# A hybrid decoder step on one core: fillers in every pause of TensorE's start, and two loads on another queue

## The chip, the cores and the metric

The kernel runs on one core of one Trainium2 chip. The metric is the time of one execution on the device, in microseconds (us), as the median of several runs. TensorE (PE) multiplies matrices, VectorE (DVE) and ScalarE (ACT) work elementwise, GpSimd (POOL) does the small rest, and the queues of SyncE (SP) and of ScalarE can issue transfers (DMA).

## The reference

One inference step of a decoder layer for a prompt of 512 rows and 32 sampled rows (8 sequences of 4), each row 1024 wide, in float32. What matters here is the front of the layer and the size of what follows:

```python
shift, scale, gate = jnp.split(jax.nn.silu(c) @ w_cond + b_cond, 3, axis=-1)
h = x * (1 + scale[:, None]) + shift[:, None]
return gate, split_columns(h @ w_in)          # w_in: 1024 x 11280
...
yA = dilated_attention(...)                   # 3 groups of 8 heads, then combined by their softmax sums
yB = gated_delta(short_conv(qkv_b), ...)      # 8 heads of 128
merged = sigmoid(g_a) * (yA @ w_branch_a) + sigmoid(g_b) * (yB @ w_branch_b)
y = LayerNorm(ALPHA * x + gate * (merged @ w_out))
```

It also returns the new key and value caches, the convolution rows and the delta states.

## The kernel before

**Products in three parts.** A float32 product of `h` with a weight tile is made of three rounded ones: each operand is split into a high part (ScalarE's copy to float32r) and a low part (VectorE's subtraction). `hhi`, `hlo` are those of `h`; `whi`, `wlo` or `hi`, `lo` those of a weight tile `wt`. One tile of `h @ w_in` is 8 blocks of 128 rows (`k`) x 3 products x 2 halves of 272 columns, into banks of PSUM called `pp` (two), or `pg` (three), `pb` (one), `pd` (two).

**The front.** `h` depends on `c`. `cT` (the transposed conditioning vectors) is loaded, ScalarE's `th` (tanh) and two instructions of VectorE make `cs` from it, which is silu(c). Then for each of the 8 blocks `k`: a group of 8 matmuls `pd<-wm,cs` with the block `wm[k]` of `w_cond`; ScalarE's copy `Y`; two small matmuls `pd<-cst,Y`, which transpose it; VectorE's `mod` adds the bias `mb` (from `bT`) and scales `xT[k]`; ScalarE's `hhi` and VectorE's `hlo` split it. As soon as a block of `h` is there, the matmuls of the first three weight tiles (`ahead`) use it, six a tile.

The loads of the front all stand in SP's queue, in this order, with their size in KB: `cT` 128, `bT` 12, `wm0` 1024, `cst` 165, `xT` 544, `wm1` 1024, `wt` 512, `wm2` 1024, `xT` 544, `wt` 512, `wm3` 1024, `wt` 512, `wm4` 1024, `xT` 544, `wm5` 1024, `wm6` 1024, `xT` 544, `wm7` 1024: 12,209 KB (12.5 MB) in all. `wm2` ends 4,433 KB (4.5 MB) into it.

**The order.** The kernel is recorded first: every operation goes into a list with its reads and writes (`Recorder.add`; all instructions therefore have one line, L707, in the profile). `Recorder.schedule` then plays the list through with costs in microseconds and, at each planned moment, gives each engine the ready operation of the best rank. What it writes down is the order of the instructions on each engine; the chip keeps to that order, and waits on semaphores for real.

**Fillers.** `Recorder.warm` puts a matmul of ones (`warm<-ones`, 128x128, float32, into a spare bank) into TensorE's order where the planner sees a pause of at least `GAP` = 0.25 us. It refuses where the planned busy time of the last 3.413 us (`heat`) is over `HEAT` = 3.0 us:

```python
heat = sum(b - max(a, at - 3.413) for a, b in busy[-400:] if b > at - 3.413)
if heat > self.HEAT:
    return None
```

**Further on.** Two things that the prediction speaks of: a `za` job (one weight tile, evacuated in two halves by ScalarE's `spare<-pp` or `zt<-pp` and VectorE's `spare<-spare,pp` or `zt<-zt,pp`, which frees the bank), and the combination of the three attention groups: weights `R` are made on VectorE and ScalarE, stored to a DRAM tile `dw`, loaded again, spread over partitions, as `wv`, and multiplied on VectorE into `ya` and `NB`. While that goes on the large caches are copied from DRAM to DRAM by the same queue (`out_kv_s<-in_cache`).

Of the kernel before, what the change touches and what calls it, by code (L numbers as in the profile page):

```python
# [245 lines left out]
class Recorder:  # L246
# [4 lines left out]
    OVER = {"ve": 0.08, "se": 0.10, "ge": 0.05}  # L251
    AGAIN = {"pe": 0.0, "ve": 0.11, "se": 0.14, "ge": 0.11, "sp": 0.0}
    HOLD = 1.0
    GAP, HEAT = 0.25, 3.0
    ENTER = {(128, 128): 0.197, (64, 128): 0.197, (64, 64): 0.142, (32, 32): 0.073, (128, 64): 0.1, (128, 32): 0.0,
             (64, 32): 0.1, (32, 128): 0.2, (32, 64): 0.1}
    ENGINES = ("pe", "ve", "se", "ge", "sp")
# [397 lines left out]
    def warm(self, wait, avail, at, best, busy, state):  # L655

        if avail or best is None or best[0] < at or best[1] == "pe" and best[0] <= at:
            return None
        if wait and wait[0][0] < at + self.GAP:
            return None  # L660
        heat = sum(b - max(a, at - 3.413) for a, b in busy[-400:] if b > at - 3.413)
        if heat > self.HEAT:
            return None
        for pool, tag in self.spare:
            key = (id(pool), tag)
            s = state.get(key)
            if not pool.open or s is None or not s["slots"] or s["wait"] or min(s["slots"]) + self.WAKE["pe"] > at:
                continue
            v = pool.tile([128, 512], F32, name="warm", tag=tag)
            v.base.bufs = pool.bufs  # L670
            self.rank, self.group = 40, None
            op = self.add("pe", "matmul", (v[:, 0:128], self.ones, self.ones), dict(start=True, stop=True))
            self.rank = 0
            t = v.base
            t.turn, t.left, t.line, t.given = {}, 1, None, True
            t.free = max(s["slots"].pop(s["slots"].index(min(s["slots"]))), pool.since)
            for x in (t, self.ones.base):
                x.pool.left += 1
            self.ones.base.left += 1
            op.left, op.banks, op.ready, op.group = 0, [t], at, None  # L680
            self.warmed = getattr(self, "warmed", 0) + 1
            return op
        return None
# [76 lines left out]
def body(ctx, tc, io):  # L760
    rec = Recorder()
    pe, ve, se, ge, sp = rec.engines()
# [94 lines left out]
    with ExitStack() as fctx:  # L857
        fr = pool(fctx, "front", 1)
        cT = fr.tile([128, KT, 32], F32, name="cT")
        sp.dma_start(cT, io["cT"])  # L860
        bT = fr.tile([128, 24], F32, name="bT")
        sp.dma_start(bT, io["bT"])
        th = fr.tile([128, KT, 32], F32, name="th")
        se.activation(th, cT, AF.Tanh, scale=0.5)
        ve.tensor_scalar(th, th, 0.5, 0.5, op0=OP.mult, op1=OP.add)
# [1164 lines left out]
    at = [0, 0, 9, 9, 18, 18, 27, 27]  # L2030
# [311 lines left out]
```

## Time and profile before

| | |
|---|---|
| median of 3 runs | 927.26 us (926.62 to 927.31) |
| the profiled execution | 929.9 us, of which the span of instructions is 928.1 us |
| TensorE busy | 907.1 us, 98% of the span |
| VectorE, ScalarE busy | 737.6 us (79%), 435.2 us (47%) |
| fillers | 17 instructions, the last before 21.5 us |
| mean granted clock of TensorE | 0.993 |

The profile is of one execution. A row of a timeline has the start and the duration in us, the engine, the line, the operation with its output and inputs, how many instructions are merged in the row, and in brackets the idle time before it with what ended it. A row of windows has, after the stretch and its length, the busy time of PE, PEld (weight loads), DVE, ACT and POOL with the number of instructions, the granted clock, the share of the DMA engines and GB/s. A float32 matmul shows as two rows.

### The profile page before, as it was taken

Reading aid. Unit: us, or ns where it says so; the run is one execution under the profiler, and the core shown is the slowest. Engines: PE = TensorE matmul, PEld = TensorE weight load, DVE = VectorE, ACT = ScalarE, POOL = GpSimd, SP = SyncE. Lnnn points to the kernel's source line nnn. Section 1 sums busy time; section 2 is a strip of 40 time slices with the busy share of each in tenths; the row PEclk is TensorE's granted clock in tenths of the full one; section 3 lists DMA queues with packets and bytes.
Section 4 is the critical chain, followed back from the end, with each engine's and each line's share of the span. In section 5 each row is a group of like instructions: output and inputs, shape, how many; then the busy total and the mean of one; then the engine's idle time right before and its main releaser. Section 6 shows DMA issues by size and latency. Waiting matters only on the chain.

```text
span 928.1 us, 20971 instructions
## 1 busy us (share of the span) xinstructions
PE 907.1 (98%) x8168; PEld 847.6 (91%) x8168; DVE 737.6 (79%) x1635; ACT 435.2 (47%) x1007; POOL 78.7 (8%) x187
## 2 busy tenths in 40 slices
PE   8999999999999999999999999999999999999895
PEld 6899999999998999998999998988999999997684
DVE  3486668587679999999999977466899989857658
ACT  3374636656355756446766445422532222245311
POOL 0131011120000130001120000020010000000000
PEclk9999999999999999999999999999999999999998
DMA  9776677477787779898779685479699999989613
GB/s 359 290 206 220 190 233 234 148 222 230 204 262 231 268 234 299 269 319 267 262 256 292 189 278 209 122 243 378 209 312 364 329 406 387 345 286 316 227 41 116
DMA packets 104569, 237.89 MB, mean 256 GB/s; under 512 B 29891, under 2 KB 61261, under 8 KB 100757
## 3 DMA queue, kind: packets, MB, share of 16 engines
q1 hardware_dynamic: 104468, 236.55, 76.2%
q8 instruction: 64, 1.05, 0.5%
q14 instruction: 37, 0.30, 0.1%
HBM read 220.49 MB, written 103.70 MB: 349 GB/s over the span
## 4 chain that ended last, share of the span: by engine, by line
PE 79%; DVE 11%; DMA 5%; ACT 2%; issue 2%; SPq 0%; DVEq 0%; ACTq 0%
PE pp L707 55%; PE pg L707 11%; PE pd L707 8%; PE pb L707 3%; DVE r L707 2%; DVE lo L707 2%; DVE slab L707 1%; DMA wt<-in_w_in 1%; DMA wm<-in_w_mod 1%; DVE tmp L707 1%; DVE Tb L707 1%; DMA wv<-dw 1%; DMA rb<-dr 1%; ACT L707 1%; DMA dO<-vr 1%
## 5 line engine op out<-in xcount | busy, mean ns | idle before, releaser
L707 PE MATMUL pp<-hhi,hi 128*128 128x272 f32 x1360 | 399.9, 294 | 2.0 <-DVE spare L707 2.0
L707 PE MATMUL pp<-hhi,lo 128*128 128x272 f32 x1360 | 401.7, 295 | 0.0
L707 PE MATMUL pp<-hlo,hi 128*128 128x272 f32 x1360 | 400.3, 294 | 0.0
L707 PEld LDWEIGHTS pp<-hhi,hi 128*128 128x128 f32 x1360 | 257.1, 189 | 4.6 <-DVE spare L707 2.3
L707 PEld LDWEIGHTS pp<-hlo,hi 128*128 128x128 f32 x1360 | 257.3, 189 | 2.2 <-issue 1.3
L707 PEld LDWEIGHTS pp<-hhi,lo 128*128 128x128 f32 x1360 | 257.0, 189 | 2.1 <-issue 1.0
L707 ACT ACTIVATE hi<-wt 128x1024 fp32r<-128x1024 f32 (+1 forms) x102 | 104.6, 1026 | 183.8 <-PE pp L707 150.9
L707 DVE TENSOR_TENSOR lo<-wt,hi 128x1024 fp32r<-128x1024 f32 (+1 forms) x102 | 119.9, 1176 | 34.9 <-ACT hi L707 34.2
L707 DVE SCALAR_TENSOR_TENSOR acc<-ext,cw,acc 128x568 f32<-128x568 f32 x72 | 57.3, 799 | 5.2 <-ACT acc L707 4.9
L707 ACT ACT_TABLE_LOAD x38 | 48.8, 1283 | 4.1 <-DVE acc L707 2.7
L707 DVE TENSOR_REDUCE slab<-slab 128x8 f32<-128x512 f32 (+2 forms) x66 | 42.7, 654 | 0.2
L707 DVE TENSOR_TENSOR slab<-slab 128x512 f32<-128x512 f32 (+1 forms) x66 | 42.8, 665 | 0.1
L707 ACT ACTIVATE P<-P,st 128x256 f32<-128x256 f32 (+1 forms) x64 | 31.2, 489 | 20.8 <-DVE st L707 20.6
L707 POOL COPY cx<-ext 128x3 f32<-128x3 f32 (+1 forms) x48 | 32.3, 703 | 70.8 <-ACT ext L707 70.7
L707 ACT ACTIVATE zt<-pp 128x272 f32<-128x272 f32 x48 | 18.7, 389 | 41.0 <-PE pp L707 32.1
L707 PE MATMUL pp<-ybl,hi 128*128 128x272 f32 x128 | 37.1, 290 | 0.0
L707 PE MATMUL pp<-ybh,lo 128*128 128x272 f32 x128 | 37.0, 289 | 0.0
L707 PE MATMUL pp<-ybh,hi 128*128 128x272 f32 x128 | 36.9, 288 | 0.0
L707 PE MATMUL pg<-k,q 128*128 128x128 f32 (+1 forms) x192 | 35.7, 309 | 0.0
L707 PEld LDWEIGHTS pg<-k,q 128*128 128x128 f32 x192 | 27.8, 191 | 3.0 <-issue 1.4
L707 ACT ACTIVATE q<-pp 64x272 f32<-64x272 f32 (+1 forms) x48 | 26.3, 549 | 8.5 <-PE pp L707 8.0
L707 DVE CUSTOM_DVE_ANT_0 P<-pg,bias 128x256 f32<-128x256 f32 (+1 forms) x64 | 24.0, 401 | 3.7 <-PE pg L707 3.3
(408 smaller groups left out, 1673.4 us busy)
## 6 DMA issues: line engine op xcount, KB each, us to landing
out_kv_s<-in_cache SPq DMA_DIRECT2D x144, 512.0 KB
wt<-in_w_in SPq DMA_DIRECT2D x88, 512.0 KB
out_kv_s<-in_cache SPq DMA_DIRECT2D x24, 496.0 KB
wm<-in_w_mod SPq DMA_DIRECT2D x8, 1024.0 KB
slab<-in_ks SPq DMA_DIRECT2D x32, 256.0 KB
slab<-in_vs SPq DMA_DIRECT2D x32, 256.0 KB
kv<-in_ks SPq DMA_DIRECT2D x16, 512.0 KB
kv<-in_vs SPq DMA_DIRECT2D x16, 512.0 KB
```

The costliest lines, as they stand in the source:

```text
L707: getattr(real[x.engine], x.name)(*map(arg, x.args), **{k: arg(v) for k, v in x.kw.items()})
```

## The change

A constant `FULL` = 17.0 is added: before 17 us of planned time, the limit on `heat` no longer holds, so that every pause of at least 0.25 us gets a filler. And the two loads of `cT` and `bT` are issued by ScalarE instead of SP.

```diff
-    GAP, HEAT = 0.25, 3.0
+    GAP, HEAT, FULL = 0.25, 3.0, 17.0
...
         heat = sum(b - max(a, at - 3.413) for a, b in busy[-400:] if b > at - 3.413)
-        if heat > self.HEAT:
+        if heat > self.HEAT and at > self.FULL:
             return None
...
         cT = fr.tile([128, KT, 32], F32, name="cT")
-        sp.dma_start(cT, io["cT"])
+        se.dma_start(cT, io["cT"])
         bT = fr.tile([128, 24], F32, name="bT")
-        sp.dma_start(bT, io["bT"])
+        se.dma_start(bT, io["bT"])
```

The planner's times move with it, and so the order of the instructions on every engine, to the end of the program. Of TensorE's matmuls only the fillers change in number: 29 instead of 17.

TensorE at the start of the program, before:

```order
L707 MATMUL warm<-ones 128x128 x8
L707 MATMUL pd<-wm,cs 32x256 x8
L707 MATMUL warm<-ones 128x128
L707 MATMUL pd<-cst,Y 128x9 x2
L707 MATMUL pd<-wm,cs 32x256 x8
L707 MATMUL warm<-ones 128x128 x4
L707 MATMUL pp<-hhi,whi 128x272 x2
L707 MATMUL warm<-ones 128x128 x2
L707 MATMUL pd<-cst,Y 128x9 x2
```

TensorE at the same place, now:

```order
L707 MATMUL warm<-ones 128x128 x12
L707 MATMUL pd<-wm,cs 32x256 x8
L707 MATMUL warm<-ones 128x128 x2
L707 MATMUL pd<-cst,Y 128x9 x2
L707 MATMUL warm<-ones 128x128 x7
L707 MATMUL pd<-wm,cs 32x256 x8
L707 MATMUL warm<-ones 128x128 x3
L707 MATMUL pp<-hhi,whi 128x272 x2
L707 MATMUL warm<-ones 128x128 x2
L707 MATMUL pd<-cst,Y 128x9 x2
```

Four more fillers stand ahead of the first group, one more behind it, seven new ones ahead of the second group, and one fewer behind that.

VectorE where the weights `R` of the attention groups are finished, before (this is near 590 us in the profile):

```order
L707 RECIPROCAL Z<-Z 128x128
L707 TENSOR_TENSOR R<-R,Z 128x256
L707 SCALAR_TENSOR_TENSOR spare<-spare,pp 128x272
L707 TENSOR_TENSOR lo<-wt,hi 128x1024
L707 SCALAR_TENSOR_TENSOR ya<-ya,spare 128x512
L707 SCALAR_TENSOR_TENSOR S<-S,etot,pd 128x128
L707 RECIPROCAL rn<-rn 128x4
L707 TENSOR_TENSOR vr<-pd,rn 128x512
L707 SCALAR_TENSOR_TENSOR zt<-zt,pp 128x272
```

VectorE at the same place, now:

```order
L707 TENSOR_TENSOR lo<-wt,hi 128x1024
L707 SCALAR_TENSOR_TENSOR spare<-spare,pp 128x272
L707 SCALAR_TENSOR_TENSOR ya<-ya,spare 128x512
L707 RECIPROCAL rn<-rn 128x4
L707 TENSOR_TENSOR vr<-pd,rn 128x512
L707 TENSOR_TENSOR R<-R 128x256
L707 SCALAR_TENSOR_TENSOR zt<-zt,pp 128x272
L707 TENSOR_TENSOR Z<-R 128x128
L707 RECIPROCAL Z<-Z 128x128
L707 TENSOR_TENSOR R<-R,Z 128x256
```

The last step of `R` stood ahead of `lo`, `ya` and `vr`; now it stands behind them and behind one `zt`.

VectorE a little later, where the products with `wv` meet the evacuation of the `za` jobs, before (near 610 us):

```order
L707 TENSOR_TENSOR ya<-ya,wv 128x4x4x32
L707 SCALAR_TENSOR_TENSOR spare<-spare,pp 128x272
L707 TENSOR_TENSOR NB<-NB,wv 128x4x4x32
L707 TENSOR_TENSOR ya<-ya,NB 128x512
L707 TENSOR_TENSOR ya<-ya,wv 128x4x4x32
L707 TENSOR_TENSOR nd<-nd,cum 128x256
L707 TENSOR_TENSOR NB<-NB,wv 128x4x4x32
L707 TENSOR_TENSOR nd<-nd,cd 128x256
L707 TENSOR_TENSOR lo<-wt,hi 128x1024
L707 SCALAR_TENSOR_TENSOR spare<-spare,pp 128x272
```

VectorE at the same place, now:

```order
L707 SCALAR_TENSOR_TENSOR spare<-spare,pp 128x272
L707 TENSOR_TENSOR nd<-nd,cum 128x256
L707 TENSOR_TENSOR nd<-nd,cd 128x256
L707 TENSOR_TENSOR ya<-ya,wv 128x4x4x32
L707 TENSOR_TENSOR lo<-wt,hi 128x1024
L707 SCALAR_TENSOR_TENSOR spare<-spare,pp 128x272
L707 TENSOR_TENSOR NB<-NB,wv 128x4x4x32
L707 SCALAR_TENSOR_TENSOR spare<-spare,pp 128x272
L707 TENSOR_TENSOR ya<-ya,NB 128x512
```

Between the first job's two evacuations (`spare<-spare,pp`) there stood three products with `wv`, a sum, two `nd` and a `lo`; now there stand two `nd`, one product with `wv` and the `lo`.

## The prediction

> **What bounds the kernel now.** I read the page's head first, then the chain of waits, then the first 20 us of TensorE in order of time, and last the two places where TensorE stops later on.
>
> From the page:
>
> ```profile
> span 928.1 us, 20971 instructions
> PE 907.1 (98%) x8168; PEld 847.6 (91%) x8168; DVE 737.6 (79%) x1635; ACT 435.2 (47%) x1007; POOL 78.7 (8%) x187
> PE 79%; DVE 11%; DMA 5%; ACT 2%; issue 2%; SPq 0%; DVEq 0%; ACTq 0%
> ```
>
> TensorE is busy for 98% of the span and holds 79% of the chain that ended last. Time is won by giving it real work earlier, or by letting it run at full speed for longer. A busy share does not say which: a filler counts as busy, and so does a matmul at half speed. So I read the start, TensorE alone in order of time (start, duration, what, count):
>
> ```profile
> 1.05 3.78 PE L707 MATMUL warm<-ones 128*128 128x128 f32 x16 [1.05 <-DVE ones L707]
> 6.94 1.94 PE L707 MATMUL pd<-wm,cs 128*32 128x256 f32 x16 [2.11 <-DMA wm<-in_w_mod]
> 9.40 0.99 PE L707 MATMUL pd<-cst,Y 128*128 128x9 f32 x4
> 11.18 1.94 PE L707 MATMUL pd<-wm,cs 128*32 128x256 f32 x16 [0.79 <-DMA wm<-in_w_mod]
> 13.05 2.08 PE L707 MATMUL warm<-ones 128*128 128x128 f32 x8
> 15.38 1.05 PE L707 MATMUL warm<-ones 128*128 128x128 f32 x4
> 16.22 0.86 PE L707 MATMUL pd<-cst,Y 128*128 128x9 f32 x4
> 16.94 0.63 PE L707 MATMUL pp<-hhi,wlo 128*128 128x272 f32 x2
> 17.75 1.07 PE L707 MATMUL pd<-wm,cs 128*32 128x256 f32 x16
> 19.38 0.61 PE L707 MATMUL pd<-cst,Y 128*128 128x9 f32 x4
> 20.81 0.61 PE L707 MATMUL warm<-ones 128*128 128x128 f32 x4
> ```
>
> Each float32 matmul leaves two rows, so x16 is eight instructions. The same group `pd<-wm,cs` takes 1.94 us at 6.94 and at 11.18 and 1.07 us at 17.75; a filler takes 0.47 us (3.78 / 8) before and 0.30 us (0.61 / 2) after. TensorE runs at about half speed until some 17.4 us, although the profile's clock column says 1.00 there. The first 3.78 us of fillers did not lift it, and then came a pause of 2.11 us. The stretch that began at 11.18 lifted it after about 6.2 us. Between 13.05 and 16.4, over 3 us went into fillers at half speed, and the third block's group only came at 17.75.
>
> When were its inputs there? Bytes moved (windows; the last column is GB/s):
>
> ```profile
> 0.00:4.00 4.00, 2.95 (x14) 2.95 (x15) 1.07 (x7) 1.70 (x2) 0.20 (x4) 1.00 0.44 101
> 4.00:8.00 4.00, 1.89 (x16) 1.22 (x19) 0.00 (x0) 0.00 (x0) 0.00 (x0) 1.00 0.99 396
> 8.00:12.00 4.00, 3.21 (x25) 1.83 (x18) 0.93 (x4) 0.89 (x2) 0.00 (x0) 1.00 1.02 428
> 28.00:32.00 4.00, 4.00 (x46) 3.06 (x38) 1.64 (x6) 1.04 (x2) 0.00 (x0) 1.00 1.02 419
> ```
>
> From 4 us on the transfers run at some 415 GB/s, all 16 engines full. In the order of issue the third block of `wm` ends 4.5 MB into the front (the sizes stand with the kernel above). 101 x 4 + 396 x 4 + 428 x 4 is 3.7 MB by 12 us, so it is complete at about 14 us, or 14.4 with the 0.4 us that a landing takes to be seen. TensorE reaches it 3.3 us later, at 17.75. Here TensorE is late, not the data, and that is the time to be won.
>
> **The change, part by part.**
>
> *The two loads move to ScalarE's queue.*
>
> ```profile
> 0.73 1.28 ACT L707 ACT_TABLE_LOAD   x1 [0.73 <-PEq L2315]
> 0.73 0.39 SPq L707 DMA_DIRECT2D cT<-in_cT  x1
> 1.19 0.41 SPq L707 DMA_DIRECT2D bT<-in_bT  x1
> 1.64 0.43 SPq L707 DMA_DIRECT2D wm<-in_w_mod  x1
> 3.56 0.42 DVE L707 TENSOR_TENSOR cs<-cT,th 128x256 f32<-128x256 f32 x1
> ```
>
> SP's first load of `wm` moves from 1.64 to 0.73, and all its later ones with it: 0.91 us at most. The 140 KB of `cT` and `bT` (256 and 24 float32 in each of 128 partitions) must still move, now at the same time: 0.35 us at 415 GB/s. So the data comes 0.56 to 0.91 us earlier; I take 0.6. On ScalarE two issues (0.39 + 0.41 us) now stand ahead of the table load of 1.28 us, so `th` cannot start before about 2.9 us (2.79 now); shared bandwidth may make that 3.3, and `cs` is then ready by some 4.5 us instead of 3.98. The first block lands at 6.94 - 0.6 = 6.3. These two issues cost nothing; should `cT` be starved for longer than 1.8 us, every microsecond more delays the first group.
>
> *More fillers.* Twelve extra in all, none after row 51 of TensorE's order: 12 instead of 8 ahead of the first group, 2 instead of 1 before its `pd<-cst,Y`, 7 new ones before the second group, 3 instead of 4 behind it, one behind the third. From 1.05 on TensorE then has no long pause. Speed rises after more than 3.78 us of work (that much did not do it) and at most 6.2 (that did): between 4.8 and 7.3 us. The 12 fillers end at 6.7 if all are slow (12 x 0.47), near 5.9 if not. The first group starts at 6.3 to 6.7 and ends at 7.4 to 8.3. Y needs 0.4, `pd<-cst,Y` 0.6: 8.4 to 9.3. Seven fillers at 0.30 end at 10.5 to 11.4; the second block's data is seen at 11.18 - 0.6 = 10.6. Its group ends at 11.7 to 12.5.
>
> Then ScalarE decides:
>
> ```profile
> 12.43 1.15 ACT L707 ACTIVATE whi<-wt 128x512 fp32r<-128x512 f32 x2 [0.28 <-DMA wt<-in_w_in]
> 13.48 0.36 ACT L707 ACTIVATE Y<-pd 128x256 f32<-128x256 f32 x1
> ```
>
> `whi` waits for a block of weights, and the second Y stands behind it in both kernels. 0.6 us earlier gives Y at 13.84 - 0.6 = 13.2. `pd<-cst,Y` at full speed (0.61) ends at 13.9, four matmuls of `pp` bring 14.6, one pause between shapes 14.8 to 14.9. The third group starts there, just as its data comes (14.4 - 0.6 = 13.8). So the front gains 17.75 - 14.9 = 2.8 us. With no lead of the loads it is 2.3, with the full 0.91 it is 3.1.
>
> The Trainium skill, "TensorE: Matmul & The Clock Gate" (Part 1, the HAM clock gate), says that the window in which the clock is decided is free-running and about 3.4 us long, so the point at which it rises differs between runs. The rows above (not after 3.78 us, but within 6.2) agree; no second run of this trace shows the spread. By that page the clock before could rise earlier in other runs than in this profile, and the gain would be smaller, about 2 us.
>
> From the rows alone the same doubt is priced so. If work that began at 11.18 lifted the clock at 15.0 (just over 3.78 us) instead of 17.4, the fillers from 13.05 end at 15.05, the next two `pp` at 15.5, two fillers at 16.05, `pd<-cst,Y` at 16.4, `pp` at 16.9: the gain against that run is 16.9 - 14.9 = 2.0. The median of three runs may hold either. I take the middle of 2.0 and 2.8: **2.4 us**.
>
> *Does the gain last?* The last block and the last matmuls that need it:
>
> ```profile
> 36.17 1.07 PE L707 MATMUL pd<-wm,cs 128*32 128x256 f32 x16
> 43.86 0.41 PE L707 MATMUL pp<-hhi,whi 128*128 128x272 f32 x2
> ```
>
> The eighth block ends 12.5 MB into the front: at 415 GB/s from 12 us (3.7 MB) that is 33.2, seen at 33.6. Now TensorE comes to it at 36.17, 2.6 us late; with loads 0.6 earlier it can come 3.2 earlier before it waits. Behind it stand 66 matmuls of other blocks (0.125 us each) before the last block's `h` is read at 43.86. So 2.4 fits, and what is late next is that eighth block. After it TensorE has work without a break.
>
> *The planner's order behind the front.* The rows differ down to the end, since each choice hangs on planned times. The work is the same: besides the twelve fillers no kind of matmul changes its count. So the term is what stalls do. Two are large:
>
> ```profile
> 613.01 0.39 PE L707 MATMUL pp<-hhi,hi 128*128 128x272 f32 x1 [2.04 <-DVE spare L707]
> 614.00:619.00 5.00, 5.00 (x30) 5.00 (x29) 0.98 (x3) 1.35 (x2) 0.23 (x1) 0.66 0.76 304
> 872.76 0.47 PE L707 MATMUL pp<-wo0h,mhi 128*128 128x512 f32 x1 [2.07 <-DVE lo L707]
> 873.00:879.00 6.00, 6.00 (x20) 4.73 (x20) 4.45 (x7) 2.38 (x4) 0.00 (x0) 0.72 0.33 117
> ```
>
> Each stops TensorE for 2 us, and then the granted clock falls (0.66 over 5 us, 0.72 over 6): 1.7 us more. One such stop is worth 3.7 us. At 872 VectorE's row that frees the bank (`lo`) stands behind three splittings of `w_out` in both orders: no change. At 613 it stands behind the products with `wv`, which come from DRAM by way of `dw` (VectorE in order of time, and one step of the chain of waits):
>
> ```profile
> 588.45 0.28 DVE L707 TENSOR_TENSOR Z<-R 128x128 f32<-128x128 f32 x1
> 588.76 0.95 DVE L707 RECIPROCAL Z<-Z 128x128 f32<-128x128 f32 x1
> 589.75 0.42 DVE L707 TENSOR_TENSOR R<-R,Z 128x256 f32<-128x256 f32 x1
> 595.11 0.44 DVE L707 SCALAR_TENSOR_TENSOR zt<-zt,pp 128x272 f32<-128x272 f32 x1 [0.81 <-ACT zt L707]
> 604.39 1.06 DVE L707 TENSOR_TENSOR ya<-ya,wv 128x512 f32<-128x512 f32 x1
> 607.09 1.07 DVE L707 TENSOR_TENSOR NB<-NB,wv 128x512 f32<-128x512 f32 x1 [1.19 <-DMA wv<-dw]
> 611.38 1.23 DVE L707 TENSOR_TENSOR lo<-wt,hi 128x1024 fp32r<-128x1024 f32 x1
> 612.51 0.44 DVE L707 SCALAR_TENSOR_TENSOR spare<-spare,pp 128x272 f32<-128x272 f32 x1
> ...
> 600.40 6.67 DMA wv<-dw
> ```
>
> In the new order only one product with `wv`, one `lo` and two `nd` stand between the two evacuations (before, three products, a sum, two `nd` and the `lo`), which would end the stop. But R is finished later: behind the `zt` of 595.11 and three more instructions of its own (0.28 + 0.95 + 0.42 us), at 597.2 instead of 590.2. From R to the first product it took at most 14.2 us (604.39 - 590.17); with fewer issues of SP between, 12 to 14. So `wv` is there at 609.2 to 611.2, and 1.06 + 1.23 + 0.44 later, at 611.9 to 613.9, `spare` is done; now it is 612.95. I take no change, with -3.7 (no stop) and +5.2 (`wv` late, worked out below) as ends.
>
> **Sum.** Profiled execution: 929.9 (span 928.1 and 1.8 around it); less 2.4 is 927.5. The median of the runs shown, 927.26, lies 2.6 under that execution; the same 2.4 off it gives 924.9.
>
> **The rivals.** A measurement of this kernel tells about 0.2%, 1.85 us, from nothing: faster is under 925.4, slower above 929.1.
>
> Small gain: TensorE is fed no faster than the loads, so only their lead is won, 0.6 to 0.9 us, or the clock rises early in both. For it: all DMA engines are full from 4 to 32 us. Against it: TensorE reached the third and the eighth block 3.3 and 2.6 us after they were there. 926.5.
>
> The stop at 613 goes as well: 927.26 - 2.4 - 3.7 = 921.2. For it: the shorter row of VectorE ahead of `spare`. Against it: R is 7 us later.
>
> Slower: at the same place `wv` lands late. Two halves are loaded one behind the other, and the longest landing in this chain took 6.67 us. If the second product gets its half that much after the first, both column halves of TensorE's next tile wait: the stop grows from 2.04 to about 5.5 us and a second slow stretch of 1.7 us follows, +5.2 in all: 930.1. It decides once the first product with `wv` starts after about 613 us instead of 611.
>
> The change doesn't do what it says: the clock stays low up to 20 us although TensorE is fed. Then the first group ends at 8.6 and its `pd<-cst,Y` at 10.6, seven fillers cost 3.3 us instead of 2.1 in front of the second group, whose end comes at 15.8; three fillers (1.4), `pp` (0.8), two fillers (0.9), `pd<-cst,Y` (0.9) and `pp` (0.8) bring 20.6 for the third group instead of 17.75: 2.9 us lost, 930.2. Against it: 6.2 us of work did lift the clock.
>
> **How the numbers follow.** Forecast (2 to 3.1 us gained, the rest even) 0.45; small gain 0.24; the stop at 613 goes 0.13; other stops come or go by a microsecond or two, result about even, 0.07; slower by `wv` 0.08; clock stays low 0.03. Faster 0.45 + 0.13 = 0.58; within 0.2% 0.24 + 0.07 = 0.31; slower 0.11. The range holds the first two, and the case without the stop down to 921.5: 921.5 to 928.0. What it leaves out is the slower cases, 0.11, and half of 921.2, 0.07.
>
> **What the changed profile would show.** `wm`'s first issue at about 0.73. TensorE's first group at 6.3 to 6.7 and the second in 1.07 us, not 1.94. The third at 14.6 to 15.3; if it starts after 16.5, the step through ScalarE's `whi` is wrong. The eighth at about 33.5. Near 610 a stop of 1 to 3 us and a granted clock under 0.8 behind it; none there means the 921 case. The prediction fails if the fillers still run in 0.47 us after 8 us, or if TensorE waits over 3 us anywhere behind the front.

## The result: 0.56% slower, and the profile after

The changed kernel takes 932.36 us (median of 4 runs, 932.03 to 933.64); the kernel before, on the same chip, 927.28 (926.62 to 928.46). The ratio is 1.0056 with an interval of 1.0038 to 1.0073. Predicted were 924.9 us and a range of 921.5 to 928.0. The profiled execution took 932.03 us, its span 930.3. The granted clock rises and falls at another moment in each run, and runs of one kernel scatter here by up to 9 us; so times below are medians, each with the ratio to runs of before on the same chip (it can differ by 0.06% from the ratio of the two medians), and a profile is one run of such a set.

The head of the page of the changed kernel, as it was shown of before:

```profile
span 930.3 us, 21015 instructions
PE 908.0 (98%) x8192; PEld 846.7 (91%) x8192; DVE 738.4 (79%) x1635; ACT 440.0 (47%) x1009; POOL 85.0 (9%) x187
PE 85%; DVE 5%; DMA 5%; ACT 3%; issue 1%; SPq 0%; DVEq 0%; ACTq 0%
```

TensorE's share of the chain rose from 79% to 85% and VectorE's fell from 11% to 5%: by this view the kernel got better. The time says otherwise, so shares are no verdict.

TensorE at the start, in order of time, after:

```profile
1.05 4.98 PE L707 MATMUL warm<-ones 128*128 128x128 f32 x24 [1.05 <-DVE ones L707]
7.81 1.07 PE L707 MATMUL pd<-wm,cs 128*32 128x256 f32 x16 [1.78 <-DVE cs L707]
9.85 1.81 PE L707 MATMUL warm<-ones 128*128 128x128 f32 x14
11.59 1.07 PE L707 MATMUL pd<-wm,cs 128*32 128x256 f32 x16
15.10 1.07 PE L707 MATMUL pd<-wm,cs 128*32 128x256 f32 x16
34.73 1.07 PE L707 MATMUL pd<-wm,cs 128*32 128x256 f32 x16 [0.16 <-DMA wm<-in_w_mod]
```

The clock is up: the first two groups take 1.07 us, not 1.94, and the third starts at 15.10 instead of 17.75, 2.65 us earlier. But the first group is late (7.81, was 6.94), and what it waits for is `cs`, no longer `wm`. The eighth group, at 34.73, is only 1.44 us earlier than before (36.17), and now it waits for its data.

How much of this the fillers did can be read from all the profiles of this document. Seven kernels, before among them, have the eight old fillers ahead of the first group; in two of these (`redraw_copies`, `front_old_order_new`) that group takes 1.07 us all the same, but the second takes 1.93 or 1.94 in all seven. So the quick first group can come without the change; the quick second one did not.

Why `cs` is late: ScalarE and VectorE at the start, after (an issue has the queue's name, ACTq):

```profile
0.73 0.41 ACTq L707 DMA_DIRECT2D cT<-in_cT  x1
6.37 0.42 ACT L707 ACTIVATE th<-cT 128x256 f32<-128x256 f32 x1 [3.43 <-DMA cT<-in_cT]
7.33 0.42 DVE L707 TENSOR_TENSOR cs<-cT,th 128x256 f32<-128x256 f32 x1
```

The DMA queues in the first 6.4 us of it (packets, MB, share of 16 engines):

```profile
q1 hardware_dynamic: 339, 1.44, 61.8%
q10 hardware_dynamic: 288, 0.14, 7.5%
```

ScalarE was free from 2.94 us and waited 3.43 us for `cT`, which was issued at 0.73 as planned. Its queue (q10) moved 0.14 MB in 288 packets of 0.5 KB on the mean, while SP's (q1) moved 339 packets of 4.2 KB. The Trainium skill, "DMA: Bandwidth & Descriptors" (Queues, rings and completion order), says that each DMA engine takes turns between the queues by packets. The trace agrees: of about as many packets, SP's queue moved ten times the bytes. Ahead of `wm` in one queue, `cT` had been whole before 2.8 us.

Behind the front: TensorE's largest group of matmuls, with the start of the first and of the last of its 1,360 instructions, of before and (second fence) of after:

```profile
L707 PE MATMUL pp<-hhi,hi x1360: 282/288/478, 50.8 to 855.1; 128*128 128x272 f32 x195
```

```profile
L707 PE MATMUL pp<-hhi,hi x1360: 282/288/479, 49.3 to 860.9; 128*128 128x272 f32 x195
```

The same 1,360 matmuls, with the same median of 288 ns, begin 1.5 us earlier, and the last starts 5.8 us later; the first `pp<-wo0h,mhi` behind them starts at 868.17 instead of 864.40, 3.8 later. The loss is between, not in the front.

The stops of TensorE behind the front, after (before: 613.01 with 2.04 us and 872.76 with 2.07):

```profile
52.75 0.66 PE L707 MATMUL pb<-cst,KQ 128*128 128x128 f32 x4 [0.64 <-ACT ext L707]
358.89 0.66 PE L707 MATMUL pb<-cst,KQ 128*128 128x128 f32 x4 [0.74 <-DVE kr L707]
404.22 0.49 PE L707 MATMUL pd<-vr,XF 128*128 128x128 f32 x2 [0.39 <-DVE XF L707]
638.74 1.08 PE L707 MATMUL pb<-S,KP 128*32 128x128 f32 x32 [0.38 <-DMA S<-in_state_delta]
707.15 0.39 PE L707 MATMUL pp<-hhi,hi 128*128 128x272 f32 x1 [0.49 <-ACT zt L707]
711.72 0.39 PE L707 MATMUL pp<-ybh,hi 128*128 128x272 f32 x1 [1.31 <-ACT zt L707]
784.11 0.39 PE L707 MATMUL pp<-hhi,hi 128*128 128x272 f32 x1 [0.49 <-ACT zt L707]
876.53 0.47 PE L707 MATMUL pp<-wo0h,mhi 128*128 128x512 f32 x1 [2.05 <-DVE lo L707]
```

The stop of 613 is gone; that of 872 stands at 876; seven smaller ones are new (one of 0.61 us at 354, in before, is gone). At 711 ScalarE has a splitting `hi` in front of the `zt` that would free the bank.

The stop of 876 is as long as that of 872 was, but the granted clock did not fall behind it (before: 0.72 over 6 us):

```profile
876.50:882.50 6.00, 5.97 (x26) 4.91 (x27) 4.84 (x8) 1.79 (x3) 0.00 (x0) 1.00 0.32 108
```

In all the profiles of this document there are 14 stops of 1.87 us or more behind 600 us, and the clock fell behind seven of them. The profile of before, from which a stop was priced, has a fall behind each of its two.

How far each kernel is behind an ideal one, worked out from all matmul starts: at time t, t less the sum of the median steps of the matmuls begun so far, fillers counted as nothing. More is worse; only differences between columns count. (The first two are before and after; the others are experiments below.)

```
   t   before  after  front_old_  f2_order  old_no_
                      order_new     _old     stops
  45    23.6    22.0     22.9       22.3     23.6
  60    23.6    23.0     23.3       22.5     23.7
 100    24.2    23.6     23.9       23.2     24.3
 250    31.0    33.3     33.6       29.9     31.0
 450    44.0    47.5     47.8       42.8     44.4
 600    52.8    56.7     57.2       51.5     53.1
 650    65.2    65.7     66.3       64.2     61.7
 725    65.8    68.9     69.4       64.9     62.3
 850    72.8    77.1     77.1       71.9     69.4
 875    77.9    81.0     81.6       76.4     71.7
```

After is 1.6 us ahead at 45 us, 0.6 at 60; 2.3 behind at 250, 3.5 at 450, 3.9 at 600. The missing stop of 613 brings it back to 0.5 behind, 650 to 725 costs 2.6, and so on. Between 100 and 600 us no one place holds the loss: sorted by pairs of neighbouring matmuls, no pair takes over 1.5 us more in the new order (`front_old_order_new`, below) than in that of before.

Nor are these 500 us lost in waits that the profile shows. Windows of before, then of `front_old_order_new`:

```profile
100.00:600.00 500.00, 498.50 (x4897) 471.88 (x4896) 418.70 (x1094) 286.70 (x716) 51.38 (x124) 1.00 0.75 239
```

```profile
100.00:600.00 500.00, 498.21 (x4859) 468.73 (x4858) 416.08 (x1090) 290.51 (x722) 57.00 (x124) 1.00 0.72 236
```

TensorE is idle for 1.5 and 1.8 us, nearly the same, yet gets 38 rows less done; at the usual 0.126 us from start to start these are 4.8 us. One difference can be counted in the rows: neighbours on TensorE have another weight shape (`128*128`, `128*64`, `128*32`, `32*32` and so on) 220 times in the new order and 193 times in that of before. By the starts of the matmuls such a change takes about 0.09 us more than a step within one shape, and 0.3 from `128*32` to `128*128`; in sum the changes cost 3.4 us more in the new order. No run took them back, so this is a count, not an experiment.

### The profile page after: what moved, and what is told of

The parts are those of the page before. It is cut to its first block, busy times and chain, and to the rows that moved or that the text cites. A ratio compares the mean times of both kernels' runs of the same rounds, so it can differ in the third digit from the quotient of the medians.

```text
span 930.3 us, 21015 instructions
## 1 busy us (share of the span) xinstructions
PE 908.0 (98%) x8192; PEld 846.7 (91%) x8192; DVE 738.4 (79%) x1635; ACT 440.0 (47%) x1009; POOL 85.0 (9%) x187
## 4 chain that ended last, share of the span: by engine, by line
PE 85%; DVE 5%; DMA 5%; ACT 3%; issue 1%; SPq 0%; DVEq 0%; ACTq 0%
PE pp L707 63%; PE pg L707 11%; PE pd L707 7%; PE pb L707 4%; DVE r L707 2%; DMA wm<-in_w_mod 2%; DMA wt<-in_w_in 1%; DMA S<-in_state_delta 1%; ACT hi L707 1%; DMA cT<-in_cT 1%; ACT L707 1%; DMA bias<-in_bias_p 1%; DVE zt L707 0%; ACT QKd L707 0%; ACT q L707 0%
## 5 line engine op out<-in xcount | busy, mean ns | idle before, releaser
L707 POOL COPY cx<-ext 128x3 f32<-128x3 f32 (+1 forms) x48 | 38.7, 836 | 78.0 <-ACT ext L707 77.9
```

The costliest lines, as they stand in the source:

```text
L707: getattr(real[x.engine], x.name)(*map(arg, x.args), **{k: arg(v) for k, v in x.kw.items()})
```

## The experiments

Three theories. *Order*: the new order of the instructions costs some 5 us by itself. *Front*: the fillers or the late `cT` cost more than they bring. *Draw*: the order is one of many that the planner could have written, each some microseconds up or down, and the change only drew another one. Postponing in an order, below, always means: moved to a later place on its own engine, the rest unchanged. A graft keeps the whole written order of one kernel and sets into it the fillers and the two loads of the other.

### Order or front, and two draws

Edits: `front_new_order_old` is the kernel before with the twelve fillers and the two loads grafted when the order is written out; `front_old_order_new` is the changed kernel with both taken back in the same way.

```diff
+        EXTRA, DROP, MOVED = {8: 4, 17: 1, 19: 7, 49: 1}, (30,), ('cT', 'bT')
...
+                if x.engine == "pe":
+                    for _ in range(EXTRA.get(place, 0)):
+                        w = self.spare[0][0].real.tile([128, 512], F32, name="warm", tag=self.spare[0][1])
+                        nc.tensor.matmul(w[:, 0:128], self.ones.real(), self.ones.real(), start=True, stop=True)
...
+                if x.name == "dma_start" and x.outs and x.outs[0].base.kw["name"] in MOVED:
+                    nc.scalar.dma_start(*map(arg, x.args), **{k: arg(v) for k, v in x.kw.items()})
```

`redraw_margin` and `redraw_copies` are the kernel before with one planner constant moved, which changes nothing but the order:

```diff
-        return 0.1 if p.transfer is None else 0.5
+        return 0.1 if p.transfer is None else 0.52
...
-MOVES = (48.0, 850.0)
+MOVES = (47.0, 850.0)
```

Expected of them:

> The order of every instruction is that of the kernel before; only the front is the new one: the 12 more fillers at the same places as in the changed kernel, and cT and bT loaded from ScalarE's queue. Theory 'order' (the front gains, and what the planner made of the rest loses): the third group of pd<-wm,cs starts near 15.1 us instead of 17.75, and the time is 1 to 2.5 us under the kernel before, 925 to 926. Theory 'front' (the fillers or the late cT cost the time): some 5 us over the kernel before, 931 to 933.

> The mirror image: the order of every instruction is that of the changed kernel, but the front is the old one: 12 fillers taken out at the places where the change put them, cT and bT back in SP's queue ahead of wm. Theory 'order': the loss stays and the front's gain is gone, so 1 to 2.5 us over the changed kernel, 933 to 935. Theory 'front': back to some 927.

> The kernel before with one number of the planner changed that has no meaning for the chip: the planned lag of a load is 0.52 instead of 0.50 us. No instruction is added or moved to another engine; only the order behind it changes. Theory 'order': the time moves by a few microseconds either way, with a size like the 5 us of the change (2 to 6 us from 927). Theory 'front': it stays within 1 us of 927.

> The kernel before, but the planned time of the first cache copy is 47 instead of 48 us (the last stays at 850). The same question as with the margin: theory 'order' 2 to 6 us from 927 either way, theory 'front' within 1 us.

| kernel | median us (range, runs) | ratio to before |
|---|---|---|
| `front_new_order_old` | 930.05 (925.26 to 934.63, 12) | 1.0014 [0.9996, 1.0032] |
| `front_old_order_new` | 933.21 (932.22 to 934.53, 6) | 1.0056 [1.0040, 1.0073] |
| `redraw_margin` | 924.71 (923.49 to 925.81, 10) | 0.9963 [0.9949, 0.9977] |
| `redraw_copies` | 934.55 (933.60 to 935.68, 6) | 1.0071 [1.0055, 1.0087] |

The new order with the old front has the whole loss (0.56%, by the ratio 5.2 us of 928.39). Constants that mean nothing for the work move the time by -0.37% and +0.71%, so 5 us is what the order alone is worth between draws. Stops of `redraw_copies`, which show where such a draw loses:

```profile
617.30 0.40 PE L707 MATMUL pp<-hhi,hi 128*128 128x272 f32 x1 [1.45 <-DVE spare L707]
624.82 0.39 PE L707 MATMUL pp<-hhi,hi 128*128 128x272 f32 x1 [1.23 <-DVE spare L707]
860.99 1.12 PE L707 MATMUL pg<-Y,cst 128*128 128x512 f32 x2 [1.15 <-ACT Y L707]
879.45 0.47 PE L707 MATMUL pp<-wo0h,mhi 128*128 128x512 f32 x1 [2.06 <-DVE lo L707]
```

`redraw_margin` has no stop of TensorE over 0.7 us behind the front.

### The parts of the front, and the stops

Edits: `fill_only_old` and `load_only_old` graft one of the two parts. `old_no_stops` and `new_no_stops` postpone a few instructions, in the orders of before and after, with

```diff
+        postpone([self.ops[7132], self.ops[7189]], self.ops[7185])  # NB<-NB,wv and lo behind spare<-spare,pp
+        postpone([self.ops[9723], self.ops[9729]], self.ops[9755])  # two wo1l behind lo<-pp,gs
...
+        postpone([self.ops[8177]], self.ops[8176])                  # ScalarE: hi behind zt<-pp
+        postpone([self.ops[9723], self.ops[9729]], self.ops[9755])
```

> The order of before on every engine and its loads on SP; only the twelve extra fillers stand at the places where the new kernel has them. Theory A (the fillers do what the prediction said, and the late cT spoilt it): cs is ready near 4.0 us again, so the first group starts when wm0 lands, 6.9 to 7.0 (not 7.8), in about 1.1 us; the second group at 11.2 to 11.4 in 1.07 us; the third at 15.0 to 15.6 instead of 17.75; the time is 2.0 to 2.6 us under that of before, near 926.0. Rival B (what the front gains does not reach the end, because the clock falls again behind the pauses or because TensorE waits for a chain of ScalarE near 53 us): the third group may be as early, but the time is within 1 us of before, 927.4 to 929.4.

> The order of before on every engine and its fillers; only cT and bT are issued by ScalarE. Theory A (cT is starved beside SP's 1 MB loads): cs is ready near 7.8 us instead of 4.0, the first group waits for cs and starts near 7.8 instead of 6.94, at half speed, and the time is 0.5 to 1.5 us longer than before, near 929.3. Rival (cT was late only because of something else in the new kernel): cs by 4.5, the first group near 6.3, 0.6 us faster, near 927.8.

> The order of before but for four of VectorE's instructions, each moved behind the evacuation that frees TensorE's bank: at the stop of 613 the product NB with wv and one splitting lo behind spare<-spare,pp, and at the stop of 872 two splittings of w_out behind the lo that empties the bank. The front is that of before. Theory order (what stands ahead of an evacuation on VectorE is worth the idle time and the low clock behind it): both stops of 2 us go, and with each the 1.7 us of low clock; 928.4 less 4.0 to 7.4 gives 921 to 924.4. Rival (VectorE is merely late, and the moved work makes the next bank late, so that the wait comes back some us later): within 1 us of before, 927.4 to 929.4.

> The changed kernel whole, but for three instructions: ScalarE's hi at 710 stands behind the zt<-pp for which TensorE waited, and two splittings of w_out stand behind the lo that empties the bank at 876. Theory order: the stop of 1.31 us at 711.7 shrinks to about 0.4 (the wait of 707.15 and 784.11, where nothing stands ahead of zt), and that of 2.05 at 876 goes with or without its 1.7 us of low clock: 932.4 less 2.9 to 4.6 gives 927.8 to 929.5, level with before, though two of the three stops that the chip shows behind the front are gone; what is left of the loss against the first kernel without stops (about 6 us) then is in small waits between 100 and 600 us. Rival (the waits come back later): 931.4 to 933.4.

| kernel | median us (range, runs) | ratio to before |
|---|---|---|
| `fill_only_old` | 928.38 (926.35 to 930.86, 12) | 1.0001 [0.9986, 1.0015] |
| `load_only_old` | 925.98 (924.47 to 930.40, 12) | 0.9973 [0.9958, 0.9987] |
| `old_no_stops` | 922.55 (921.68 to 923.42, 5) | 0.9942 [0.9929, 0.9956] |
| `new_no_stops` | 929.75 (928.17 to 931.82, 12) | 1.0019 [1.0006, 1.0033] |

Four instructions of VectorE at other places are worth 5.4 us, with the front of before. VectorE at 610 us in `old_no_stops` (its lines of code have other numbers, since some were added), and then two stretches by windows:

```profile
609.54 0.42 DVE L725 TENSOR_TENSOR nd<-nd,cd 128x256 f32<-128x256 f32 x1
609.89 0.43 DVE L725 SCALAR_TENSOR_TENSOR spare<-spare,pp 128x272 f32<-128x272 f32 x1
610.23 1.05 DVE L725 TENSOR_TENSOR NB<-NB,wv 128x512 f32<-128x512 f32 x1
611.21 1.20 DVE L725 TENSOR_TENSOR lo<-wt,hi 128x1024 fp32r<-128x1024 f32 x1
```

```profile
614.00:619.00 5.00, 5.00 (x39) 4.89 (x38) 3.38 (x7) 1.75 (x3) 2.02 (x5) 1.00 0.96 344
869.00:875.00 6.00, 6.00 (x28) 4.86 (x27) 5.63 (x9) 1.80 (x3) 0.00 (x0) 1.00 0.41 153
```

`spare` now ends at 610.32 instead of 612.95. Both stops are gone, and so are the low clocks behind them (1.00 and 1.00, before 0.66 and 0.72). The prediction gave a stop a price of 2.0 + 1.7 us; for two that is at most 7.4, and 5.4 were won, which fits a clock that falls behind some stops and not behind others. The wait did not come back later.

`new_no_stops` has lost its large stops too (3.4 us better than after by the two ratios), but stays 0.77% above `old_no_stops`: 7 us that no stop over 0.8 us shows. This fits the spread loss of the table above.

`fill_only_old` won nothing in its median. Its profile has a reason:

```profile
6.97 1.07 PE L719 MATMUL pd<-wm,cs 128*32 128x256 f32 x16
9.21 3.75 PE L712 MATMUL warm<-ones 128*128 128x128 f32 x14
12.89 1.07 PE L719 MATMUL pd<-wm,cs 128*32 128x256 f32 x16
16.40 1.07 PE L719 MATMUL pd<-wm,cs 128*32 128x256 f32 x16
```

Seven fillers take 3.75 us where the changed kernel's take 1.81. That is no low clock (the groups beside it take 1.07 us): the graft put all its fillers into one bank, and each waited for the one before (TensorE idle 2.3 us in nine waits for `warm`). The planner's fillers take turns between two banks. So every graft that adds fillers, up to here and in the next group, prices them too high.

### The front on a kernel without stops

Runs of `old_no_stops` scatter by less than 2 us, so it makes a better ground. Edits: the same grafts on it (fillers, loads, both), and for `no_stops_front_bias` one more:

```diff
+        postpone([self.ops[1711]], self.ops[801])  # ScalarE: bias<-bias behind the four QKd
```

> The kernel without the stops of 613 and 872 (922.55 us, or 0.58% under before), plus the twelve extra fillers; the loads stay on SP. Theory eaten at 53 (what the front gains ends at ScalarE's bias<-bias, which waits for a transfer that lands near 49 us whatever the front does, and stands ahead of the ext copies that empty TensorE's bank): third group up to 1.4 us earlier, a wait for ext of 0.3 to 0.7 us near 53, and the time equal: ratio to before 0.993 to 0.9955. Rival (the front's 2.4 us are real, and the stops hid them): 920.1, ratio 0.9916.

> The kernel without the stops of 613 and 872, plus cT and bT issued by ScalarE; the fillers are those of before. In the order with the stops this edit gave a ratio of 0.9973, though the trace shows the first group 0.9 us later and the work done at 40 us ahead by only 0.2. Theory phase (that gain came from where the clock's fall met the stops, not from the front): no gain here, ratio to before 0.993 to 0.9955. Rival (the earlier wm loads are worth 2.3 us by themselves): 920.2, ratio 0.9917.

> The kernel without the stops of 613 and 872, plus the whole change of the front: the twelve fillers and cT and bT issued by ScalarE. Theory eaten at 53: cs near 7.3 to 7.8 us, the third group 0.5 to 2.7 us earlier than 17.75, a wait for ext of 0.3 to 0.7 us near 53, ratio to before 0.993 to 0.9955. Rival (2.4 us arrive): 920.1, ratio 0.9916. Second rival (the front costs, as the 1.0014 in the order with the stops may mean): 923.5 to 924.5, ratio 0.995 to 0.9965.

> As the one before, but ScalarE's bias<-bias stands behind the four QKd that follow the ext copies, so that its wait for the transfer holds no ext. Theory eaten at 53: the wait for ext near 53 us goes, the work done at 60 us is ahead of the kernel without stops by what the front had gained at 45 us (0.5 us in the older order, more where the clock rises earlier), and the time is 0.4 to 1.5 us under that of the front without this edit: 921 to 922.2, ratio 0.9918 to 0.9935. Rival (another chain of ScalarE or the next transfer is late in its place): no change by this edit.

| kernel | median us (range, runs) | ratio to before |
|---|---|---|
| `no_stops_fill` | 924.42 (923.50 to 925.14, 5) | 0.9957 [0.9942, 0.9972] |
| `no_stops_load` | 923.11 (921.43 to 923.66, 5) | 0.9938 [0.9921, 0.9956] |
| `no_stops_front` | 927.09 (923.13 to 929.70, 12) | 0.9982 [0.9964, 1.0000] |
| `no_stops_front_bias` | 925.83 (923.16 to 930.25, 12) | 0.9979 [0.9960, 0.9998] |

`no_stops_load` equals `old_no_stops`: the 0.27% of `load_only_old` were not in the front. The kernels with both parts fall into two heaps, 923.1 to 924.4 and 926.8 to 930.3 us (11 runs and 13). The profile of `no_stops_front_bias` (930.25 us) is one of the upper heap:

```profile
8.07 1.93 PE L738 MATMUL pd<-wm,cs 128*32 128x256 f32 x16 [1.48 <-DVE cs L738]
12.08 5.90 PE L731 MATMUL warm<-ones 128*128 128x128 f32 x14
17.91 1.94 PE L738 MATMUL pd<-wm,cs 128*32 128x256 f32 x16
23.07 1.07 PE L738 MATMUL pd<-wm,cs 128*32 128x256 f32 x16
```

Here the clock had risen near 4.4 us, and from the wait of 1.48 us for `cs` on it was low until 21.5. This is the rival "the clock stays low", worse than it was worked out (23.07 for the third group, not 20.6), since these fillers also wait for each other. The fillers stand in TensorE's order, so at a low clock real work waits behind them.

### The fillers in their own banks

The graft mended: the changed kernel's 29 fillers by place and bank, so that their waits are the same as its own.

```diff
+        MOVED, FILLS, place = ('cT', 'bT'), {}, 0
+        for at, tag in [(0, 'b'), (0, 'g'), (0, 'b'),
...
+            FILLS.setdefault(at, []).append(tag)
+        banks = {tag: pool for pool, tag in self.spare}
...
+                    if x.outs[0].base.kw["name"] == "warm":
+                        continue
+                    for tag in FILLS.get(place, ()):
+                        o = banks[tag].real.tile([128, 512], F32, name="warm", tag=tag)
```

`f2_order_old` is before with the whole front; `f2_ns_fill` and `f2_ns_front` are `old_no_stops` with the fillers and with the whole front; `f2_ns_fill_bias` has the fillers and the postponed `bias`.

> The order of before on every engine, its two stops included; the whole change of the front: all 29 fillers at the places and in the banks of the changed kernel, so that none waits for the one before it, and cT and bT issued by ScalarE. (In front_new_order_old the twelve grafted fillers all went into one bank and waited for each other: seven took 3.74 us, in the changed kernel 1.56.) Theory eaten at 53: first group near 7.8, third near 15.1, a wait for ext of 0.6 us near 53, and 0.3 to 0.9 us won: ratio to before 0.999 to 0.9997. Rival (the 2.4 us of the prediction arrive): ratio 0.9974. Second rival (the clock stays low in some runs): ratio over 1.001 and runs that scatter by over 6 us.

> The kernel without the stops of 613 and 872 (ratio to before 0.9942), with all 29 fillers in the banks of the changed kernel; the loads on SP. Theory eaten at 53: first group 7.0 in 1.07 us, second near 11.0, third 14.3 to 14.8, a wait for ext near 53, ratio 0.993 to 0.9942. Rival (the gain arrives): 0.991 to 0.992.

> The same with cT and bT issued by ScalarE, so the whole change of the front without the two stops. Theory eaten at 53: cs near 7.4 to 7.8, third group near 15.1, ratio 0.993 to 0.9945. Rival (the late cs leaves a pause of over 1 us in which the clock stays low in some runs, and the fillers behind it then cost twice): ratio over 0.995 and a scatter of over 4 us.

> As f2_ns_fill, but ScalarE's bias<-bias stands behind the four QKd that follow the ext copies, so its wait for a transfer (it lands near 49 us) holds no ext. Theory eaten at 53: no wait of TensorE for ext near 53, and the lead that the front has at 45 us (1 to 2 us) is still there at 60: ratio 0.992 to 0.9932. Rival (the next chain is late in its place): as f2_ns_fill.

| kernel | median us (range, runs) | ratio to before |
|---|---|---|
| `f2_order_old` | 927.13 (925.41 to 930.88, 12) | 1.0001 [0.9986, 1.0015] |
| `f2_ns_fill` | 923.48 (922.43 to 925.55, 8) | 0.9959 [0.9943, 0.9975] |
| `f2_ns_front` | 923.98 (921.25 to 925.04, 8) | 0.9954 [0.9936, 0.9971] |
| `f2_ns_fill_bias` | 923.16 (923.08 to 924.84, 7) | 0.9951 [0.9932, 0.9969] |

In the order of before the whole front is worth nothing (1.0001); without stops none of the three beats `old_no_stops` (0.9942), though the intervals overlap. The front of `f2_ns_front`, same fillers, same loads as after:

```profile
7.76 1.54 PE L739 MATMUL pd<-wm,cs 128*32 128x256 f32 x16 [1.89 <-DVE cs L739]
10.96 3.33 PE L734 MATMUL warm<-ones 128*128 128x128 f32 x14
14.22 1.45 PE L739 MATMUL pd<-wm,cs 128*32 128x256 f32 x16
18.12 1.07 PE L739 MATMUL pd<-wm,cs 128*32 128x256 f32 x16
```

Its first two groups lie between 1.07 and 1.93 us: the clock went down in the first, behind the wait for `cs`, and came back in the second. Over the six profiles with the whole changed front (after, `new_no_stops`, `f2_order_old`, `f2_ns_front`, and the two below) the third group starts at 15.10, 15.09, 16.45, 18.12, 18.55 and 15.18, on the mean 16.42, and the eighth at 35.45; over the five with the old one (before, `old_no_stops`, `redraw_margin`, `redraw_copies`, `front_old_order_new`) at 17.39 and 35.94. The mean gain is 1.0 us at the third block and 0.5 at the eighth.

The eighth block has a second limit. With the loads on SP as before, TensorE waits for that block's data wherever it comes early enough; first `redraw_copies`, then `f2_ns_fill`:

```profile
35.42 1.07 PE L707 MATMUL pd<-wm,cs 128*32 128x256 f32 x16 [0.21 <-DMA wm<-in_w_mod]
```

```profile
35.17 1.07 PE L736 MATMUL pd<-wm,cs 128*32 128x256 f32 x16 [0.16 <-DMA wm<-in_w_mod]
```

Five profiles show this wait, and it ends at 35.2 to 35.8. So the data was not there at 33.6, and before had 0.4 to 1.0 us to win at this block, not 2.6.

The theory of the wait near 53 us is half right. In after the front's lead does end there. ScalarE's row of before, then that of after, then a piece of after's chain of waits (start, duration, what):

```profile
49.03 1.06 ACT L707 ACTIVATE bias<-bias 128x1024 f32<-128x1024 f32 x1 [0.46 <-DMA bias<-in_bias_p]
```

```profile
48.67 1.06 ACT L707 ACTIVATE bias<-bias 128x1024 f32<-128x1024 f32 x1 [1.68 <-DMA bias<-in_bias_p]
```

```profile
43.60 5.05 DMA bias<-in_bias_p
```

The transfer of `bias` lands 0.4 us earlier at most, whatever TensorE gained, and the `ext` copies behind it free TensorE's bank. But with `bias` out of the way the time stays; the next chain is late in its place (`f2_ns_fill_bias`, a row that has no wait in `old_no_stops`):

```profile
63.51 0.27 PE L737 MATMUL pb<-cst,rc 128*8 128x128 f32 x1 [0.74 <-DVE rc L737]
```

### Is the changed front to blame for the order?

Edits: the changed kernel with the two constants of the redraws.

> The changed kernel with its 29 fillers and its loads, and the planner's margin 0.5 set to 0.52, as in redraw_margin. Theory draw (the new order is one of many, and each is worth some microseconds up or down by where its stops fall): anywhere between 922 and 935, and not near 932.4; the profile then has other stops behind 100 us than 707, 711, 784 and 876, and the same front as the changed kernel (third group near 15.1). Rival (the changed front itself makes the order worse): 931 to 934 or slower.

> The changed kernel, and the start of the copies in the plan moved from 48 to 47 us, as in redraw_copies. Theory draw: between 922 and 935, unlike after_margin. Rival: 931 to 934 or slower, like after_margin.

`after_margin` takes 932.13 us (929.51 to 934.30, 7 runs), ratio 1.0046 [1.0029, 1.0062]; `after_copies` 928.58 (925.43 to 931.25, 12 runs), 1.0007 [0.9991, 1.0023]. The same constants had moved the kernel before to 0.9963 and 1.0071. So the sign turns: by 0.52 the changed kernel loses 0.8% against its old-front twin, by 47 it gains 0.6%. Neither front has the good orders for itself. Three draws a side (means 1.0011 and 1.0036) are too few to exclude a lean of the new front, since `after_margin` came out like after, as the rival said.

## Why the prediction was wrong

**The step that failed: "The planner's order behind the front", taken as 0 with ends of -3.7 and +5.2.** It measured +5.2 by the ratio (`front_old_order_new`), the upper end, but by another mechanism. I priced only what could be seen as a stop, at 613 and 872, and argued that equal work means an equal sum. At both I was half right: 872 stayed; at 613 `wv` did come later than before (first product 610.95, was 604.39; that this lies inside the 609.2 to 611.2 worked out is luck, since `R` was ready at 600.9, not 597.2, and took 10.0 us from there, not 12 to 14), and the stop went all the same: only one product stood ahead of `spare`, which ended at 614.48, and TensorE itself came 3.9 us later than before. The rival without the stop was to win 3.7 us; here TensorE had lost as much on the way to it, by what the term had no place for: 3.9 us by 600 us, the front's lead taken off, and 2.6 more from 650 to 725. Equal work did not take equal time: up to 600 us TensorE is hardly more idle, and of the 4.8 us between 100 and 600 us the 27 more changes of weight shape account for 3.4. Two redraws that cost nothing but a rebuild of the order show a spread of -3.4 to +6.6 us by their ratios; as a term of the sum this is 0 with a range of about 5 us both ways, and the chance of slower should have been well above 0.11 (near 0.4, as far as so few draws tell).

**The front, 2.4 us: mis-sized, measured 0 (1.0001 [0.9986, 1.0015]).** Four of its steps:

- "These two issues cost nothing", `cs` by 4.5: it came at 7.75. The bandwidth share was taken by bytes (0.35 us); the queues share by packets. The clause "should `cT` be starved for longer than 1.8 us" was the case, and by it the first group came at 7.81 instead of 6.3 to 6.7.
- The fillers lifted the clock in the profile of after as forecast (second group 1.07 us, third at 15.10, inside 14.6 to 15.3), but not in other runs (18.12, 18.55). Seven profiles have a pause of 1.5 to 2.1 us that the late `cs` opened behind fillers that had lifted the clock; it fell behind four of these. "More than 3.78 us (that much did not do it)" was read from one run: in two of seven profiles that much did lift the clock for the first group.
- "The eighth block ... seen at 33.6", so 2.6 us late: in other profiles its data came at 35.2 to 35.8 with the old loads, and at 34.7 in after. The bytes in the order of issue were counted rightly, but the last block was whole only when loads issued behind it had moved too (13.3 MB by 35.4 us in `redraw_copies`, not 12.5).
- "After it TensorE has work without a break": the eighth group came at 34.73, not near 33.5, and waited for its data; and ScalarE's `bias` holds the next bank until 53. The rival of the small gain, 0.6 to 0.9 us, was nearer to what the front is worth.

**What held:** SP's first `wm` issue at 0.73 (row in the trace of after), the second `Y` behind ScalarE's `whi` done at 13.21 (forecast 13.2), and the stop of 872, which stayed. The price of 3.7 us for a stop held only where the clock falls behind it: two cost 5.4 us (`old_no_stops`), not 7.4.

**Open:** why `load_only_old` won 0.27% where the stops are and nothing where they are not; whether an order with fewer changes of weight shape would win the 3.4 us back, and what the rest of the loss between 100 and 600 us is.

The best kernel found is `old_no_stops`: 922.55 us, ratio 0.9942 to before, with neither the fillers nor the moved loads.

## What to carry to other kernels

Where a planner writes the order, an edit at the start redraws everything behind it: build two or three meaningless redraws first, and take their spread as the uncertainty of any forecast, or freeze the order to measure the edit itself. On a full engine a stop of 2 us is worth finding by its row: name what stands ahead of the instruction that frees the bank, and move that. Equal work in another order is not equal time: count how often the shape of the weights changes. A small load that starts a chain should stay ahead of the large ones in their own queue.

## What the hardware showed

- Two queues share the DMA engines by packets: `cT`, issued at 0.73, was there at 6.37 us; by 6.4 us its queue had moved 288 packets (0.14 MB) and the other 339 (1.44 MB).
- The clock can fall after pauses of 1.5 to 2.1 us (0.66 over 5 us after the stop of 2.04 us; 0.72 after 2.07), and need not: 1.00 after the stop of 2.05 in after. The Trainium skill, "TensorE: Matmul & The Clock Gate" (Part 1, the HAM clock gate), has it fall after at least an idle window of about 3.4 us; here shorter pauses do it, and the measurement decides. The same front keeps its clock in one run and loses it in another.
- Behind 600 us it depends on where the stop lies. A low clock that rises again lasts 3.41 us or a multiple of it in every trace, so stretches of 3.41 us can be counted from one change of the clock. In before the stretch ahead of the fall holds 1.86 us of the stop, and the clock is 0.50 in the next; in after (second fence) two stretches share the stop of 2.05 us, and the clock stays at 1.00:

```profile
611.15:614.56 3.41, 1.55 (x12) 1.55 (x13) 3.36 (x6) 0.70 (x2) 1.22 (x1) 1.00 0.42 112
614.56:617.98 3.42, 3.42 (x17) 3.42 (x16) 0.00 (x0) 0.54 (x1) 0.00 (x0) 0.50 0.99 404
```

```profile
872.04:875.45 3.41, 2.44 (x11) 1.65 (x9) 3.41 (x4) 2.69 (x4) 0.00 (x0) 1.00 0.64 211
875.45:878.86 3.41, 2.33 (x10) 1.97 (x11) 3.36 (x7) 0.84 (x1) 0.00 (x0) 1.00 0.56 207
```

- Of the 14 stops, the seven with a fall have 1.86 us or more of idle time in one such stretch, the seven without have 1.52 or less. In the front this bound does not hold (1.78 us without a fall in after; 1.48 with one in `no_stops_front_bias`).
- Matmuls that go into one bank one behind the other, each waiting for the last, take about 0.54 us a filler (3.75 / 7); in turns between two banks 0.26 (1.81 / 7).
